# Which rows a partition owns: blocks of 512 consecutive rows against 64 consecutive rows for each partition, in an RMSNorm with SiLU

## The chip, the core and the metric

The kernel runs on one core of one Trainium2 chip. The metric is the device time of one execution in microseconds (us). Smaller is better.

## The reference

The input x has 8 × 1024 rows of 2048 float32 numbers, gamma has 2048, and the output has the shape of x.

```python
rms = np.sqrt(np.mean(x ** 2, axis=-1, keepdims=True) + eps)
out = gamma * x / rms
return (out * (1 / (1 + np.exp(-out)))).astype(np.float32)
```

Each row stands by itself: the mean of its squares gives one factor, the row is multiplied by that factor and by gamma, and SiLU is taken of the product. x and the output have 8192 × 2048 × 4 bytes = 67.1 MB each, and all of it has to be moved once.

## The kernel before

The 8192 rows are cut into nblk = 16 blocks of 512 rows. A block is a tile `xt` of 128 partitions with J = 4 rows on each, that is 8192 float32 numbers or 32 KB for a partition and 4 MB for the tile. Lines 34 to 36 say which rows these are: by the pattern `(b p j) d -> b p (j d)` block b holds rows 512b to 512b + 511, and partition p of it holds rows 512b + 4p to 512b + 4p + 3. So the 4 MB of a block lie in one piece in DRAM, and the 32 KB of partition p + 1 follow those of partition p.

Six tiles exist (BUFS = 6, line 33). Each is loaded, worked on in place and stored from the same place:

- `load(b)`, line 54: one DMA from x to the tile, issued from ScalarE's queue. The first six are issued at the start. Block s of the others is issued inside `squares_scalar(s - 2)`, behind its first Square (line 69), and can start when block s - 6 has been stored, since it takes over that tile.
- `squares_scalar` (line 65) and `squares_vector` (line 73) sum the squares of the four rows, one or two of them on ScalarE and the rest on VectorE.
- `root` (line 82, ScalarE) and `invert` (line 87, VectorE) make the factor of each row.
- `multiply`, line 92: four VectorE instructions multiply a row by its factor and gamma, in place.
- `silu`, line 98: two ScalarE instructions of two rows each, in place; then `store`, line 102, issues one DMA from the tile to the output on SyncE's queue.

The order of the instructions is written out by hand in the loop at line 125; the squares of block b + 1 stand around the product of block b. The last block goes by lines 149 to 156, with four separate SiLU instructions and one store. There is nothing on TensorE but the spreading of gamma over the partitions at the start (line 114). The arithmetic addresses tiles only, never DRAM; the names `xb` and `ob` appear in lines 54 and 102 alone.

Of the kernel before, what the change touches and what calls it, by code (L numbers as in the profile page):

```python
# [1 line left out]

# [4 lines left out]

ACT = mybir.ActivationFunctionType
ALU = mybir.AluOpType


@with_exitstack
def kernel(
    ctx: ExitStack,
    tc: tile.TileContext,
    x: bass.AP,
    gamma: bass.AP,
    eps: bass.AP,
    out: bass.AP,
):  # L20

    nc = tc.nc
    P = nc.NUM_PARTITIONS
    f32 = mybir.dt.float32
    x2 = x.flatten_outer_dims()
    o2 = out.flatten_outer_dims()  # L30
    n, d = x2.shape
    J = 4
    BUFS = 6
    nblk = n // (P * J)
    xb = x2.rearrange("(b p j) d -> b p (j d)", p=P, j=J)
    ob = o2.rearrange("(b p j) d -> b p (j d)", p=P, j=J)

    singles = ctx.enter_context(tc.tile_pool(name="singles", bufs=1))
    pool = ctx.enter_context(tc.tile_pool(name="pool", bufs=BUFS))
    small = ctx.enter_context(tc.tile_pool(name="small", bufs=2))  # L40
    psum = ctx.enter_context(tc.tile_pool(name="psum", bufs=1, space=bass.MemoryType.PSUM))

    Q = 4
    w = d // Q
    g = singles.tile([P, d], f32)
    eps_t = singles.tile([P, 1], f32)
    ones = singles.tile([P, P], f32)
    junk_a = psum.tile([P, d], f32, name="junk_a")
    junk_v = psum.tile([P, d], f32, name="junk_v")
    blocks, sss, rmss, rstds = {}, {}, {}, {}  # L50

    def load(b):
        xt = pool.tile([P, J * d], f32, name="xt")
        nc.scalar.dma_start(out=xt, in_=xb[b])  # L54
        blocks[b] = xt

    def row(b, j):
        return blocks[b][:, j * d:(j + 1) * d]

    def squares_scalar(b, loads=()):  # L60


        sss[b] = small.tile([P, J], f32, name="ss")
        for j in range(share(b)):
            nc.scalar.activation(out=junk_a, in_=row(b, j), func=ACT.Square,  # L65
                                 accum_out=sss[b][:, j:j + 1])
            if j == 0:
                for s in loads:
                    load(s)

    def squares_vector(b):
        for j in range(share(b), J):
            nc.vector.tensor_tensor_reduce(  # L73
                out=junk_v, in0=row(b, j), in1=row(b, j), scale=1.0, scalar=0.0,
                op0=ALU.mult, op1=ALU.add, accum_out=sss[b][:, j:j + 1])

    def share(b):
        return 1 if 4 <= b <= 12 and b % 2 == 0 else 2

    def root(b):  # L80
        rms = small.tile([P, J], f32, name="rms")
        nc.scalar.activation(out=rms, in_=sss.pop(b), func=ACT.Sqrt, scale=1.0 / d, bias=eps_t)  # L82
        rmss[b] = rms

    def invert(b):
        rstd = small.tile([P, J], f32, name="rstd")
        nc.vector.reciprocal(out=rstd, in_=rmss.pop(b))  # L87
        rstds[b] = rstd

    def multiply(b):  # L90
        for j in range(J):
            nc.vector.scalar_tensor_tensor(out=row(b, j), in0=row(b, j), scalar=rstds[b][:, j:j + 1],  # L92
                                           in1=g, op0=ALU.mult, op1=ALU.mult)

    def silu(b):
        for h in range(0, J, 2):
            cols = slice(h * d, (h + 2) * d)
            nc.scalar.activation(out=blocks[b][:, cols], in_=blocks[b][:, cols], func=ACT.Silu)  # L98
        store(b)

    def store(b):
        nc.sync.dma_start(out=ob[b], in_=blocks[b])

    with tc.manual_schedule():

        for b in range(BUFS):
            load(b)
        nc.vector.memset(ones, 1.0)  # L108
        nc.vector.memset(eps_t, float(eps))
        nc.scalar.activation(out=junk_a[:, 0:1], in_=ones[:, 0:1], func=ACT.Square)  # L110
        nc.sync.dma_start(out=g[0:1, :], in_=bass.AP(tensor=gamma.tensor, offset=gamma.offset, ap=[[d, 1], [1, d]]))
        for c in range(Q):
            cols = slice(c * w, (c + 1) * w)
            nc.tensor.matmul(junk_v[:, cols], ones[0:1, :], g[0:1, cols], start=True, stop=True)  # L114
        nc.vector.tensor_copy(out=g, in_=junk_v)  # L115

        last = nblk - 1
        SOON = 3  # L120
        squares_scalar(0)
        squares_vector(0)
        root(0)
        invert(0)
        for b in range(last):
            loads = [b + 3] if BUFS <= b + 3 < nblk else []
            if b < SOON:
                multiply(b)
                squares_scalar(b + 1, loads)
                silu(b)  # L130
                squares_vector(b + 1)
                root(b + 1)
            elif b < last - 1:
                squares_scalar(b + 1, loads)
                squares_vector(b + 1)
                root(b + 1)
                multiply(b)
                silu(b)
            else:
                multiply(b)  # L140
                squares_scalar(b + 1)
                silu(b)
                squares_vector(b + 1)
                root(b + 1)
            if b + 1 < last:
                invert(b + 1)


        for j in range(J):
            if j == J // 2:  # L150
                invert(last)
            nc.vector.tensor_mul(out=row(last, j), in0=row(last, j), in1=g)  # L152
        for j in range(J):
            nc.scalar.activation(out=row(last, j), in_=row(last, j), func=ACT.Silu,  # L154
                                 scale=rstds[last][:, j:j + 1])
        store(last)


# [1 line left out]
_INS = ['x', 'gamma', 'eps']  # L160
_OUTS = [((8, 1024, 2048), 'float32')]

_NUMBERS = {'eps': 9.999999747378752e-06}


# [26 lines left out]
```

## Time and profile before

| | |
|---|---|
| median of 3 runs | 316.96 us (316.75 to 317.02) |
| span of the profiled execution, first to last instruction | 315.0 us |
| median less span: what lies around it | 1.9 us |
| VectorE busy | 235.3 us (75%) |
| ScalarE busy | 213.8 us (68%) |
| DMA packets | 4612, 134.24 MB, mean 426 GB/s |
| loads: issue to landing, median | 38.7 us |
| stores: issue to landing, median | 28.6 us |

The span is cut into 40 slices in the page. In the rows of these slices a digit is the busy share in tenths, and 9 means 90% or more. The row DMA is the mean busy share of the core's 16 DMA engines. DMA queue q10 carries the loads (ScalarE's queue), q1 the stores and gamma (SyncE's queue). A DMA packet is what one DMA engine moves in one go; a block's DMA consists of 128 packets of 32 KB and 16 small ones that signal its end. In the table of windows each row is a stretch of time from the start of the span, with the busy time of each engine in it, the granted TensorE clock, the busy share of the DMA engines and the rate.

### The profile page before, as it was taken

The numbers are of one execution on the slowest core, as the hardware profiler recorded it, in microseconds if no ns is written. First come the engines' busy times: TensorE is split into PE (matmuls) and PEld (weight loads), VectorE is DVE, ScalarE is ACT, GpSimd is POOL, SyncE is SP. The second block draws the span as 40 slices with busy tenths as digits, with TensorE's granted clock in tenths as the row PEclk, the third lists the DMA queues.
The fourth block names the chain that finished last, engine by engine and source line by source line (L and its number), as shares of the span: only waits on it lengthen the run. The fifth ranks groups of instructions, "written<-read, shape, count | busy, mean of one in ns | idle before, by whom it ended". The sixth has DMA issues, their size and how long they took to land.

```text
span 315.0 us, 437 instructions
## 1 busy us (share of the span) xinstructions
PE 7.2 (2%) x8; PEld 2.5 (1%) x8; DVE 235.3 (75%) x157; ACT 213.8 (68%) x136; POOL 0.2 (0%) x4
## 2 busy tenths in 40 slices
PE   6200000000000000000000000000000000000000
PEld 3000000000000000000000000000000000000000
DVE  0679597979995795957959489593996939999600
ACT  1349998972799258782687727877288768779910
POOL 0000000000000000000000000000000000000000
DMA  8999999999999999999999999999999999999996
GB/s 334 399 466 399 399 466 399 466 399 466 399 467 404 459 416 449 420 445 420 445 420 445 420 445 420 445 424 445 420 445 429 437 429 437 429 437 433 433 433 300
DMA packets 4612, 134.24 MB, mean 426 GB/s; under 512 B 513, under 2 KB 513, under 8 KB 513
## 3 DMA queue, kind: packets, MB, share of 16 engines
q10 hardware_dynamic: 2304, 67.11, 49.8%
q1 hardware_dynamic: 2306, 67.12, 49.4%
q14 instruction: 2, 0.02, 0.0%
HBM read 67.12 MB, written 67.11 MB: 426 GB/s over the span
## 4 chain that ended last, share of the span: by engine, by line
DMA 68%; DVE 14%; ACT 11%; issue 2%; ACTq 1%; DVEq 0%
DMA xt<-in_x_dram 68%; DVE xt L92 9%; DVE junk_v L73 5%; ACT xt L98 4%; ACT junk_a L65 3%; ACT xt L154 2%; ACT L82 1%; ACTq L187 1%; ACT L154 0%; ACT L98 0%; ACT rms L82 0%; DVE ss L73 0%; DVE rstd L87 0%; ACTq L54 0%; ACTq L82 0%
## 5 line engine op out<-in xcount | busy, mean ns | idle before, releaser
L92 DVE SCALAR_TENSOR_TENSOR xt<-xt,rstd,g 128x2048 f32<-128x2048 f32 x60 | 137.0, 2345 | 0.1
L98 ACT ACTIVATE xt<-xt 128x4096 f32<-128x4096 f32 x30 | 108.3, 3615 | 27.0 <-DVE xt L92 27.0
L73 DVE CUSTOM_DVE_ANT_0 junk_v<-xt 128x2048 f32<-128x2048 f32 x37 | 85.1, 2299 | 43.0 <-DMA xt<-in_x_dram 42.3
L65 ACT ACTIVATE junk_a<-xt 128x2048 f32<-128x2048 f32 x27 | 50.6, 1876 | 22.8 <-DMA xt<-in_x_dram 22.5
L82 ACT ACT_TABLE_LOAD x15 | 19.2, 1283 | 27.4 <-DVE ss L73 27.3
L98 ACT ACT_TABLE_LOAD x14 | 18.0, 1283 | 0.2
L87 DVE RECIPROCAL rstd<-rms 128x4 f32<-128x4 f32 x16 | 2.7, 171 | 8.4 <-ACT rms L82 8.4
L152 DVE TENSOR_TENSOR xt<-xt,g 128x2048 f32<-128x2048 f32 x4 | 8.9, 2279 | 0.0
L115 DVE COPY g<-junk_v 128x2048 f32<-128x2048 f32 x1 | 2.3, 2292 | 8.6 <-PE junk_v L114 8.6
L82 ACT ACTIVATE rms<-ss,eps_t 128x4 f32<-128x4 f32 x16 | 4.8, 297 | 5.7 <-DVE ss L73 5.5
L154 ACT ACTIVATE xt<-xt,rstd 128x2048 f32<-128x2048 f32 x4 | 7.7, 1990 | 0.0
L114 PE MATMUL junk_v<-g,ones 1*128 1x512 f32 x8 | 7.2, 1073 | 2.4 <-DMA g<-in_gamma_dram 2.4
L73 DVE DVE_READ_ACCUMULATOR2_ANT ss<- 128x1 f32 x37 | 5.2, 140 | 0.0
L65 ACT ACTIVATION_READ_ACCUMULATOR junk_a<-xt 128x1 f32 x27 | 5.0, 186 | 0.0
L110 ACT ACT_TABLE_LOAD x1 | 1.3, 1283 | 3.7 <-issue 3.7
L114 PEld LDWEIGHTS junk_v<-g,ones 1*128 1x128 f32 x8 | 2.5, 326 | 5.5 <-issue 5.5
L154 ACT ACT_TABLE_LOAD x1 | 1.3, 1283 | 0.0
L108 DVE MEMSET ones<- 128x128 f32 x1 | 0.2, 165 | 0.8 <-PEq L173 0.8
L110 ACT ACTIVATE junk_a<-ones 128x1 f32<-128x1 f32 x1 | 0.2, 174 | 0.0
L173 POOL MEMSET const-bfloat16-1.0<- 128x1 bf16 x1 | 0.1, 103 | 0.0
L173 POOL MEMSET const-uint8-127<- 128x1 uint8 x1 | 0.1, 103 | 0.0
L173 POOL MEMSET const-float32-0.0<- 128x1 f32 x1 | 0.1, 99 | 0.2 <-issue 0.2
(2 smaller groups left out, 0.2 us busy)
## 6 DMA issues: line engine op xcount, KB each, us to landing
xt<-in_x_dram ACTq DMA_DIRECT2D x16, 4096.0 KB, 38.7
out_dram<-xt SPq DMA_DIRECT2D x16, 4096.0 KB, 28.6
g<-in_gamma_dram SPq DMA_DIRECT2D x1, 8.0 KB
```

Of the source, the lines that this page charges most:

```text
L65: nc.scalar.activation(out=junk_a, in_=row(b, j), func=ACT.Square, accum_out=sss[b][:, j:j + 1])
L73: nc.vector.tensor_tensor_reduce(out=junk_v, in0=row(b, j), in1=row(b, j), scale=1.0, scalar=0.0, op0=ALU.mult, op1=ALU.add, accum_out=sss ...
L82: nc.scalar.activation(out=rms, in_=sss.pop(b), func=ACT.Sqrt, scale=1.0 / d, bias=eps_t)
L87: nc.vector.reciprocal(out=rstd, in_=rmss.pop(b))
L92: nc.vector.scalar_tensor_tensor(out=row(b, j), in0=row(b, j), scalar=rstds[b][:, j:j + 1], in1=g, op0=ALU.mult, op1=ALU.mult)
L98: nc.scalar.activation(out=blocks[b][:, cols], in_=blocks[b][:, cols], func=ACT.Silu)
L110: nc.scalar.activation(out=junk_a[:, 0:1], in_=ones[:, 0:1], func=ACT.Square)
L114: nc.tensor.matmul(junk_v[:, cols], ones[0:1, :], g[0:1, cols], start=True, stop=True)
L115: nc.vector.tensor_copy(out=g, in_=junk_v)
L152: nc.vector.tensor_mul(out=row(last, j), in0=row(last, j), in1=g)
L154: nc.scalar.activation(out=row(last, j), in_=row(last, j), func=ACT.Silu, scale=rstds[last][:, j:j + 1])
L187: with _tile.TileContext(nc) as tc:
```

## The change

Two lines change. In both patterns the letter p moves to the front, so partition p owns rows 64p to 64p + 63 of x and of the output, and block b takes rows 64p + 4b to 64p + 4b + 3 from it. A block still has 4 rows or 32 KB on each partition, each partition's 32 KB are still one run, and there are still 16 blocks. The runs of neighbouring partitions of one block now lie 64 rows × 8 KB = 512 KB apart; the 32 KB that follow a partition's run belong to the same partition in the next block.

```diff
     J = 4
     BUFS = 6
     nblk = n // (P * J)
-    xb = x2.rearrange("(b p j) d -> b p (j d)", p=P, j=J)
-    ob = o2.rearrange("(b p j) d -> b p (j d)", p=P, j=J)
+    xb = x2.rearrange("(p b j) d -> b p (j d)", p=P, j=J)
+    ob = o2.rearrange("(p b j) d -> b p (j d)", p=P, j=J)
```

## The prediction, made before the changed kernel ran

> **What bounds the kernel now.** I read the 40 slices of the page first.
>
> ```profile
> DVE  0679597979995795957959489593996939999600
> ACT  1349998972799258782687727877288768779910
> ...
> DMA  8999999999999999999999999999999999999996
> ```
>
> VectorE and ScalarE have gaps all through. The DMA engines have none: every slice but the first and the last is full. Then the queues and the bytes:
>
> ```profile
> DMA packets 4612, 134.24 MB, mean 426 GB/s; under 512 B 513, under 2 KB 513, under 8 KB 513
> ## 3 DMA queue, kind: packets, MB, share of 16 engines
> q10 hardware_dynamic: 2304, 67.11, 49.8%
> q1 hardware_dynamic: 2306, 67.12, 49.4%
> ```
>
> The shares of the two queues add up to 99.2% of 16 engines for 315 us. A queue has 16 × 128 = 2048 packets of 32 KB and 16 × 16 = 256 tiny ones. So a load packet takes 0.498 × 16 × 315.0 / 2048 = 1.226 us and a store packet 0.494 × 16 × 315.0 / 2048 = 1.216 us. The trace's packet records, read one by one, say it more sharply: the mean of the loads is 1.2234 us, of the stores 1.2135 us, and more than eight in ten of either kind stand at 1.213 us, which is 32,768 B / 1.2135 us = 27.0 GB/s for one engine and 432 GB/s for 16. At nearly every moment from 2 to 313 us, 15 or 16 packets are in the air.
>
> Third, the windows, to see where this rate isn't reached, and the work that lies beside it:
>
> ```profile
> core 0: us, PE busy (x) PEld busy (x) DVE busy (x) ACT busy (x) POOL busy (x), PEclk, DMA share, GB/s
> 2.00:12.00 10.00, 7.16 (x8) 2.49 (x8) 2.29 (x1) 1.46 (x2) 0.00 (x0) 1.00 0.91 387
> 12.00:32.00 20.00, 0.00 (x0) 0.00 (x0) 17.02 (x12) 14.76 (x13) 0.00 (x0) 1.00 1.03 444
> 32.00:44.00 12.00, 0.00 (x0) 0.00 (x0) 8.71 (x7) 11.91 (x9) 0.00 (x0) 1.00 0.97 396
> 100.00:140.00 40.00, 0.00 (x0) 0.00 (x0) 29.95 (x20) 26.88 (x17) 0.00 (x0) 1.00 1.00 434
> 220.00:260.00 40.00, 0.00 (x0) 0.00 (x0) 30.23 (x21) 26.48 (x17) 0.00 (x0) 1.00 1.00 433
> ```
>
> Loads alone (12:32) and loads mixed with stores (100:140) both run at about 435 GB/s. (A packet counts where it is recorded, so a short window can be off by some per cent either way.) Two stretches are slow. By the packet records, 16 packets of the first block, one for each engine, take 1.25 to 2.25 us, which lifts the block's mean to 1.299 us. Where the first store joins the loads, at 36 to 38 us, 21 load packets take 1.28 to 1.89 us, and block 3, loaded then, has a mean of 1.293 us. The stores that join there stand at 1.213 us.
>
> The chain of waits is the last view; this is the middle of it:
>
> ```profile
> 66.81 37.73 DMA xt<-in_x_dram
> 104.56 38.95 DMA xt<-in_x_dram
> 143.54 38.66 DMA xt<-in_x_dram
> 182.23 38.68 DMA xt<-in_x_dram
> ```
>
> A load lands 38.7 us after its issue. A block's load and a block's store take 2 × 8 × 1.2135 = 19.4 us of an engine, so a load has about a block's load and store queued ahead of it. The compute engines wait for data, and the queues are never dry.
>
> **The sum before.** An engine moves 128 load packets and 128 store packets. First packet at 1.75 us; 128 × (1.2234 + 1.2135) = 311.9 us; from the last packet's end at 313.70 to the end of the span at 315.03, 1.3 us. Together 1.75 + 311.9 + 1.3 = 315.0, the span of this execution. The median of the runs, 316.96, lies 1.93 above the span, and I carry those 1.93 along.
>
> **The change part by part.** Instructions, semaphores, tiles, order and issues: nothing is added, removed or moved. A load is issued in 0.33 us and a store in 0.33 us by the trace, 16 of each, and stays so. The runs are 32 KB before and after; that the trace shows 2048 packets of 32 KB to a queue, although a block of before is one piece of 4 MB, says that the packets are already cut by partition. So I count the same 4096 data packets, at no cost.
>
> What changes is the DRAM address of each packet, thus perhaps its duration. The compute beside it covers any lengthening: in 40 us, 2.07 blocks, VectorE is busy 29.95 us, so it needs 14.5 us of a block's 19.4 and longer packets only give it more rest. Nor does a later landing start a new wait: loads are issued two blocks ahead and the queue they stand in would be the bound still. If packets became *shorter*, VectorE would be next, at 14.5 us a block, a quarter away. So the whole price is 128 × (lengthening of a load + lengthening of a store).
>
> No row of before shows runs 512 KB apart, so this price is bounded from both sides.
> - Below: a packet at 1.2135 us is the fastest any block had. If every load came to it, the gain would be 128 × (1.2234 − 1.2135) = 1.3 us. That needs the cold start and the joining of the stores to go away, which no address explains; a gain much under that is not excluded.
> - No price: in the steady state 16 engines, loads from x and stores to the output beside each other, stand at 1.213 us without scatter. The runs that they hold at one time are already whole multiples of 32 KB apart.
> - Above: the slowest block of loads in the trace, 1.299 us. All loads at that: 128 × (1.299 − 1.2234) = 9.7 us. Stores as well: 128 × (1.299 − 1.2135) = 10.9 us more, 20.6 us together.
>
> For stores I take no lengthening: those that met slowed loads at 36 to 38 us stayed at 1.213. For loads I take the middle of 1.2234 and 1.299, 1.261 us. The steady state isn't a near row, since there the runs of a block are neighbours in DRAM, and the slow blocks aren't, since in them one packet or two out of eight is long and the others are as always. That is 128 × 0.0378 = 4.8 us, and 316.96 + 4.8 = **321.8 us**.
>
> A rule speaks against this change. The Trainium skill, "DMA: Bandwidth & Descriptors", in "Latency and other measured facts", reports copies of tiles of 128 partitions whose rows lie a large power of two apart: 207 GB/s per direction at 512 KiB, 164 at 2 MiB, 103 at 4 MiB, and 214 when the pitch is padded by 4 KiB. It calls its explanation, that streams in step fall on the same channels of the memory, an inference. By its ratio of 214 to 207 the time would be an estimated 316.96 × 1.034 = 327.7 us; by the steady rows above it would not move. No row of this trace shows the pitch, so no run here shows it yet.
>
> **The rivals.**
>
> *Loads and stores both lengthen.* The new addresses are the same for both directions. For it: nothing in the change favours loads. Against it: the stores of before kept their time where loads lost theirs. From 326.6 (all loads at 1.299) to 337.6 us (stores too), more if packets get longer than the slowest block of before; the mark is a store mean above 1.23 us.
>
> *Nothing moves (not slower).* The bound is the DMA engine's own 27.0 GB/s, and the memory behind it delivers in any order of addresses without holding an engine up. For it: the exact 1.213 us of nearly all packets, in loads alone and in loads with stores, means that the engines and not the memory set the pace, so there is room before the memory counts. It decides as long as the mean packet lengthens by under 0.63 / 256 = 2.5 ns. Then 317.0 us.
>
> *A little faster.* The joining of the stores at 36 us and the cold start lose 1.3 us together. If the new addresses remove them, 315.7 us. Against it: both are bound to a moment, not to an address, and half of it must go before it can be told.
>
> *The change doesn't do what it says*, in that packets are cut otherwise than by partition: it would show in another packet count. I give it no chance of its own.
>
> **How the numbers follow.** The lean to a loss comes from the rows: nearly all packets stand at their floor, so new addresses can lengthen them and hardly shorten them; the trace has packets up to 1 us over it, and a mean of 2.5 ns over it would be told already. About 0.2% (0.63 us) is what a measurement of this kernel can tell from no change. Loads lengthen, 317.6 to 326.6 us: 0.53. Both lengthen, above 326.6: 0.18. Nothing moves: 0.22. Faster: 0.07. So slower 0.71, same 0.22, faster 0.07. The range starts at 316.3, the lower edge of no change, and ends at 332.1, the middle of the second case: left out are the 0.07 of faster and somewhat over half of 0.18, about 0.18 in all. The forecast case's own range is 317.6 to 326.6.
>
> **What would show it.** The page after should have 4612 packets, 134.24 MB, and DMA slices of 9 throughout. If I am right, q10's share of the engines rises above q1's: 1.261 against 1.2135, or about 50.4% to 48.5% of a span near 320; the windows from 100 to 260 us fall from 434 to some 425 GB/s; VectorE's and ScalarE's busy times stay at 235 and 214 us. If the windows stay at 434, nothing moved. If q1's share rises as well, both lengthen. Slices of the DMA row below 9 in the middle would say that the queues ran dry, which none of my cases has. A rate above 434 would make the whole reading wrong, for the engine's pace then was no floor.

## The result: 1.1% slower, and the profile after

The changed kernel takes 320.32 us (median of 4 runs, 319.68 to 321.78) against 316.99 us for the kernel before beside it: a ratio of 1.0112, 95% interval 1.0097 to 1.0128. The profiled execution took 320.55 us with a span of 318.8 us, 3.7 us more than the span before.

The page of the changed kernel, in the rows that were read of the kernel before (40 slices, bytes, queues):

```profile
DVE  0579597979796595956969479594895939999600
ACT  1249998971797358782587827867278768679920
...
DMA  8999999999999999999999999999999999999995
...
DMA packets 4612, 134.24 MB, mean 421 GB/s; under 512 B 513, under 2 KB 513, under 8 KB 513
## 3 DMA queue, kind: packets, MB, share of 16 engines
q10 hardware_dynamic: 2304, 67.11, 49.7%
q1 hardware_dynamic: 2306, 67.12, 48.8%
```

The packets and bytes are the same to the last one, and the DMA engines are as full as before. The two shares hardly moved, but they are shares of a longer span: a load packet is now 0.497 × 16 × 318.8 / 2048 = 1.238 us, a store packet 0.488 × 16 × 318.8 / 2048 = 1.215 us. The packet records (here and below those of one execution of each kernel) say 1.2377 and 1.2139 us, against 1.2234 and 1.2135 before. So loads got longer and stores hardly.

The windows of the changed kernel (stretch, its length, busy time of PE, PEld, DVE, ACT and POOL, granted clock, DMA share, GB/s):

```profile
40.00:80.00 40.00, 0.00 (x0) 0.00 (x0) 36.42 (x25) 28.75 (x20) 0.00 (x0) 1.00 1.00 426
80.00:120.00 40.00, 0.00 (x0) 0.00 (x0) 32.07 (x22) 27.72 (x17) 0.00 (x0) 1.00 1.00 431
120.00:160.00 40.00, 0.00 (x0) 0.00 (x0) 30.82 (x22) 26.96 (x17) 0.00 (x0) 1.00 1.01 432
160.00:200.00 40.00, 0.00 (x0) 0.00 (x0) 30.97 (x21) 27.11 (x17) 0.00 (x0) 1.00 1.00 431
200.00:240.00 40.00, 0.00 (x0) 0.00 (x0) 30.64 (x21) 26.19 (x17) 0.00 (x0) 1.00 1.00 432
240.00:280.00 40.00, 0.00 (x0) 0.00 (x0) 30.49 (x22) 30.71 (x19) 0.00 (x0) 1.00 1.00 433
295.00:305.00 10.00, 0.00 (x0) 0.00 (x0) 5.10 (x4) 9.46 (x7) 0.00 (x0) 1.00 0.94 406
```

Two of the same windows of the kernel before:

```profile
40.00:80.00 40.00, 0.00 (x0) 0.00 (x0) 36.42 (x26) 28.34 (x20) 0.00 (x0) 1.00 1.00 433
295.00:305.00 10.00, 0.00 (x0) 0.00 (x0) 1.28 (x1) 5.68 (x4) 0.00 (x0) 1.00 1.02 442
```

The loss isn't spread evenly. From 40 to 80 us the rate is 426 GB/s, and by 240 it is back at 433; the kernel before had 432 or 433 in every one of these windows from 40 to 280 us. The packet records give the same by load blocks. The table below has the mean length of a load packet of each block in ns; the excess is what the 2048 load packets take over 1.213 us each, the length of nearly all packets, divided by 16 engines.

| | block 0 | 1 and 2 | 3 | 4 | 5 | 6 to 10 | 11 to 15 | excess |
|---|---|---|---|---|---|---|---|---|
| before | 1299 | 1213 | 1293 | 1213 | 1213 | 1213 | 1213 | 1.33 us |
| after | 1307 | 1213 | 1346 | 1271 | 1235 | 1219 to 1234 | 1216 to 1224 | 3.16 us |

Blocks 1 and 2 are loaded while no store is under way, and are untouched. The loss begins in block 3, where the first store joins, and fades. Block 3 is long before as well, and in the kernel with 256 KB below, which loses no time, it has 1351 ns; what sets the changed kernel apart is the blocks from 4 on, which hold 1.34 of the 1.83 us that the excess grew by.

One thing more stands in the records. The excess rose by 1.83 us an engine, the span by 3.7. A DMA is done when the last of the engines is, and the engines no longer end together. (The records don't name the engine; a packet is put to the engine whose packet ended just before it.) Before, their last packets end from 312.95 to 313.70 us, 313.23 on the mean; after, from 315.12 to 317.57, 315.72 on the mean. The mean end moved by 2.5 us (most of it the 1.83 of excess, and pauses of 0.2 to 0.9 us on half of the engines), the last end by 3.87. The window from 295 to 305 us, with a DMA share of 0.94, has a part of the pauses in it: six engines that were ahead had emptied their queues when the last store was issued, at 304.5 us, two more did before its first packets started at 305.4. That issue itself is late because the last load landed at 282.8 us instead of 279.0; the 21.7 us of work between that landing and the issue are the same in both. The slowest engine had packets queued all the time.

### The profile page after: what moved, and what is told of

Its sections match the earlier page's. It is cut to its first block, busy times and chain, and to the rows that moved or that the text cites. A ratio compares the mean times of both kernels' runs of the same rounds, so it can differ in the third digit from the quotient of the medians.

```text
span 318.8 us, 437 instructions
## 1 busy us (share of the span) xinstructions
PE 7.2 (2%) x8; PEld 2.5 (1%) x8; DVE 235.3 (74%) x157; ACT 213.7 (67%) x136; POOL 0.2 (0%) x4
## 2 busy tenths in 40 slices
DMA packets 4612, 134.24 MB, mean 421 GB/s; under 512 B 513, under 2 KB 513, under 8 KB 513
## 4 chain that ended last, share of the span: by engine, by line
DMA 68%; DVE 14%; ACT 11%; issue 2%; ACTq 1%; DVEq 0%
DMA xt<-in_x_dram 68%; DVE xt L92 9%; DVE junk_v L73 5%; ACT xt L98 4%; ACT junk_a L65 3%; ACT xt L154 2%; ACT L82 1%; ACTq L187 1%; ACT L154 0%; ACT L98 0%; ACT rms L82 0%; DVE ss L73 0%; DVE rstd L87 0%; ACTq L54 0%; ACTq L82 0%
```

## The experiments

Three theories went in. A: runs of one block at a distance of 512 KB hold each other up, in either direction. B: it takes loads and stores that meet at the same places, so both patterns. C: any jump of an engine's addresses between packets costs. In the results "late excess" is the excess of load packets from 45 us on, after the first store has joined: 0.00 us an engine before, 1.34 after. Each ratio is to the kernel before, run beside it (medians 316.91 to 317.00 us); the changed kernel itself was not run again beside these.

**One direction alone: load_far.**

```diff
-    ob = o2.rearrange("(p b j) d -> b p (j d)", p=P, j=J)
+    ob = o2.rearrange("(b p j) d -> b p (j d)", p=P, j=J)
```

> Loads go by the new pattern, stores by the old one; each row is computed as before but written to another place of the output, so the rows come out in another order. Theory A (the pitch of 512 KB: runs of one block at such a distance hold each other up, in either direction, and the loads show it): the load packets lengthen by about half of what they do with both changed (block 3 about 1.32 us, blocks 4 to 8 about 1.22 to 1.24) and the time is about 318.6 us. Theory B (it is loads and stores that meet at the same places, which takes both patterns): load packets as before from block 4 on (1.213 us), 317.0 us. Theory C (what costs is that a load engine jumps 512 KB between packets): all of the loss, 320.3 us.

Measured: 318.72 us, ratio 1.0056 (1.0044 to 1.0068). The share of its load queue, and a span of 316.6 us, give 0.498 × 16 × 316.6 / 2048 = 1.232 us for a load packet; by the records 1.2309, and 1.2135 for stores. Its queues:

```profile
q10 hardware_dynamic: 2304, 67.11, 49.8%
q1 hardware_dynamic: 2306, 67.12, 49.1%
```

**The other alone: store_far.**

```diff
-    xb = x2.rearrange("(p b j) d -> b p (j d)", p=P, j=J)
+    xb = x2.rearrange("(b p j) d -> b p (j d)", p=P, j=J)
```

> Stores go by the new pattern, loads by the old one; the rows come out in another order. Theory A: about half of the loss, 318.6 us, shown by load packets of blocks 3 to 8, since loads wait and stores do not. Theory B: 317.0 us. Theory C: loads as before, 317.0 us, store packets at 1.2135 us.

Measured: 318.19 us, ratio 1.0035 (1.0021 to 1.0049), with one of its six runs, 317.12 us, as fast as the kernel before. Its queues:

```profile
q10 hardware_dynamic: 2304, 67.11, 49.7%
q1 hardware_dynamic: 2306, 67.12, 49.2%
```

Load packets take 1.2260 us by the records, stores 1.2135. The mean alone doesn't tell, since the kernel with 256 KB below has 1.2261 us and loses nothing. But 12 load packets after 45 us take 1.23 to 1.64 us, where the kernel before has none, although only the stores' addresses changed. So load packets carry the loss whichever direction is spread.

By time, theory A was close (318.6 expected twice) and B and C fall. By the packets A missed and B has a part: the late excess is 0.19 us with loads spread and 0.13 with stores spread, far less than half of 1.34, and blocks 4 to 8 of load_far have means of 1.214 to 1.220 us where A had 1.22 to 1.24. So most of the late lengthening takes both. (Not all: in load_far 22 packets of blocks 1 and 2, loaded before any store, take 1.23 to 1.32 us.) The times still rise by 1.7 and 1.2 us. With loads spread, the engines end 1.1 us later than before on the mean; 0.95 us of that is excess, 0.56 of it in block 3, and the slowest engine ends 1.1 us behind the mean, at 315.40 us. With stores spread, the rise is the work of single engines: the engines end at 313.52 us on the mean, 0.3 us later than before; but one of them, with four long load packets of 1.48 to 1.64 us between 155 and 275 us, ends at 315.15 us, and the span follows it.

**Another distance: pitch256 and pitch480.** In the first, two groups of 4096 rows, so that runs lie 256 KB apart:

```diff
-    xb = x2.rearrange("(p b j) d -> b p (j d)", p=P, j=J)
-    ob = o2.rearrange("(p b j) d -> b p (j d)", p=P, j=J)
+    C = 2
+    xb = x2.rearrange("(c p b j) d -> c b p (j d)", c=C, p=P, j=J)
+    xb = [xb[c, b] for c in range(C) for b in range(nblk // C)]
+    ob = o2.rearrange("(c p b j) d -> c b p (j d)", c=C, p=P, j=J)
+    ob = [ob[c, b] for c in range(C) for b in range(nblk // C)]
```

> Both patterns with two groups of 4096 rows, in each of which a partition owns 32 consecutive rows: runs of a block are 256 KB apart instead of 512 KB, all else as in the changed kernel. Theories A and B (distance in powers of two decides): a smaller loss, between 317.0 and 319 us, load mean between 1.2234 and 1.2377. Theory C (any jump costs): 320.3 us as at 512 KB.

In the second, 60 rows a partition, 480 KB:

```diff
-    xb = x2.rearrange("(p b j) d -> b p (j d)", p=P, j=J)
+    R = (nblk - 1) * P * J
+    xb = x2[0:R, :].rearrange("(p b j) d -> b p (j d)", p=P, j=J)
+    xb = [xb[b] for b in range(nblk - 1)] + [x2[R:n, :].rearrange("(p j) d -> p (j d)", p=P, j=J)]
...
```

> Both patterns with 60 consecutive rows a partition for the first 15 blocks (runs of a block 480 KB apart, not a power of two), and the last block in one piece. Theories A and B: the loss is gone, 317.0 us, load packets of blocks 4 to 14 at 1.213 us. Theory C: 320 us, load packets long as at 512 KB.

Measured: 317.03 us at 256 KB (ratio 1.0004, 0.9995 to 1.0013) and 316.91 us at 480 KB (0.9997, 0.9988 to 1.0005). No load packet after 45 us is longer than 1.23 us in either; after the change there are 98. From the page of the 480 KB kernel, bytes and queues:

```profile
DMA packets 4612, 134.24 MB, mean 426 GB/s; under 512 B 513, under 2 KB 513, under 8 KB 513
## 3 DMA queue, kind: packets, MB, share of 16 engines
q10 hardware_dynamic: 2304, 67.11, 49.8%
q1 hardware_dynamic: 2306, 67.12, 49.4%
```

These are the lines of the kernel before, digit for digit. The runs of a block lie 480 KB apart here and nothing is lost, so C is out, and so is a large distance by itself: 480 KB costs nothing, 512 KB does. That 512 KB costs because it is a power of two isn't shown, since 256 KB is one as well and is free. This is the clearest pair of the study. Neither is faster than the kernel before, whose engines already run packet on packet.

**Out of step: stagger.**

```diff
+    late = singles.tile([P, 1792], f32)
     with tc.manual_schedule():
+        for start, count in ((0, 8), (8, 8), (32, 4), (36, 4), (64, 2)):
+            nc.sync.dma_start(out=late[start:start + count, :], in_=x2[start:start + count, 0:1792])
```

> The changed kernel with five small DMAs ahead of everything on SyncE's queue (7 KB rows of x to a tile that nothing reads; 8, 8, 4, 4 and 2 partitions). They should keep 8 of the 16 DMA engines busy for 0, 4 for about 0.5, 2 for about 1.0 and 2 for about 1.3 us longer than the others, so that the engines don't walk their runs in step. Theory A in its form with step (engines in step collide, and each collision sets them apart, which is why the loss of the changed kernel fades from 1.06 us in load block 3 to 0.02 in block 15): the load excess from 45 us on, 1.34 us an engine in the changed kernel, falls to under 0.7; the time still carries up to 1.3 us of the added DMAs, so 318.5 to 320 us. If step doesn't matter (the fading has another cause): excess from 45 us on stays at 1.2 to 1.5, time 320.5 to 322 us.

Measured: 321.76 us, ratio 1.0166 (1.0143 to 1.0190); the runs lie between 321.2 and 323.7 us, and the profiled one is one of the two longest, 323.50 us. The engines were apart: they finish load block 2 over 2.4 us, against 0.9 in the changed kernel. The late excess is 1.45 us, not under 0.7, and 0.58 us of excess on stores came with it; the engines end from 314.65 to 320.43 us. The form of theory A in which engines in step collide, and a collision sets them apart, is not borne out. It doesn't fade here either: load block 12 still has a mean of 1.246 us. Why the loss of the changed kernel fades stays open.

**Larger distances: halves512, halves1m, quarters2m, and a control, halvesnear.** To get more than 512 KB, a block was cut into two or four DMAs of 64 or 32 partitions:

```diff
-    xb = x2.rearrange("(p b j) d -> b p (j d)", p=P, j=J)
+    H = 2
+    xb = x2.rearrange("(q h b j) d -> b h q (j d)", h=H, q=P // H, j=J)
...
-        nc.scalar.dma_start(out=xt, in_=xb[b])
+        for h in range(H):
+            nc.scalar.dma_start(out=xt[h * (P // H):(h + 1) * (P // H), :], in_=xb[b, h])
```

with `(h q b j)` for halves512, `(b h q j)` for halvesnear and H = 4 for quarters2m, and the stores likewise.

> Control for the next: every load and store is issued as two DMAs of 64 partitions each (2 MB), with the rows of the changed kernel, so runs of one DMA lie 512 KB apart. If the cut in two costs nothing, theory A gives 320.3 us as in the changed kernel, give or take 1 us since engines now take other partitions.

> Two DMAs of 64 partitions as in the control, but partition q of the first half and partition q of the second own neighbouring 64-row pieces, so runs of one DMA lie 1 MB apart. Theory A: a larger loss than at 512 KB, since 256 KB gave none and 512 KB gave 3.3 us: 323 to 335 us, load packets longer through all blocks. If the 512 KB loss were the whole effect of leaving the old order: the same as the control.

> Four DMAs of 32 partitions each, partition owners dealt out so that runs of one DMA lie 2 MB apart. Theory A: a larger loss again, 330 to 410 us. By the Trainium skill (DMA: Bandwidth & Descriptors, Latency and other measured facts), 164 GB/s per direction at 2 MiB against 214 would be an estimated 413 us. If the loss doesn't grow with the distance: 320 to 321 us.

> Control for the kernels cut into DMAs of 64 and 32 partitions: the rows of the kernel before, each load and store issued as two DMAs of 64 partitions, so runs of one DMA lie 32 KB apart. If the cut itself made 450 us of them (two engines then share what one had on the side of the tile: load packets of 2.5 us alone): 440 to 455 us here too. If the distance made it: about 317 us.

Measured: 450.36 us at 512 KB (440.22 to 482.48), 444.97 at 1 MB (439.43 to 451.06), 466.52 at 2 MB (462.06 to 483.12), and 451.08 us (447.82 to 454.91) in the control with runs 32 KB apart. So the cut makes the 450 us and not the distance; the control answers it, and these kernels say nothing on whether a larger distance costs more in whole DMAs. (The cut in four has no control of its own.) The windows of halvesnear, loads alone:

```profile
12.00:32.00 20.00, 0.00 (x0) 0.00 (x0) 4.89 (x5) 0.00 (x0) 0.00 (x0) 1.00 1.01 208
32.00:44.00 12.00, 0.00 (x0) 0.00 (x0) 0.00 (x0) 0.00 (x0) 0.00 (x0) 1.00 1.02 213
```

The engines are full and move half as much: a load packet of 32 KB takes 2.53 us there instead of 1.213.

**The transfers by themselves: copy_near, copy_far, copy_far16.** All the arithmetic on x is left out of both kernels; copy_far16 has J = 2 and BUFS = 12:

```diff
-        last = nblk - 1
...
-        store(last)
+        for b in range(nblk):
+            store(b)
+            if b + BUFS < nblk:
+                load(b + BUFS)
```

> The kernel before without its arithmetic: each block is stored as it was loaded, so the output is x itself. The same 4096 packets of 32 KB. Stores join at about 13 us. The DMA engines stay the bound: 316 to 317.5 us, load packets from block 2 on at 1.213 us.

> The changed kernel without its arithmetic (output is x). If the loss is the memory's and the engines' own (theory A): 1 to 6 us above copy_near, with long load packets and stores at 1.2135. If it takes the compute's timing of stores (rival D: the moments at which stores are issued, late and singly, make the collisions): within 0.7 us of copy_near. The Trainium skill's 207 against 214 GB/s per direction (DMA: Bandwidth & Descriptors, Latency and other measured facts) would make copy_near's time 3.4% longer, an estimated 327 us.

> As copy_far, with runs of 16 KB (two rows) instead of 32 KB, 32 blocks of 2 MB and 12 tiles; the distance stays 512 KB. If each start of a run can collide: about twice the loss of copy_far. If the loss goes by bytes: the same as copy_far, give or take 1 us.

Measured: 317.06 us (ratio 1.0004, 0.9995 to 1.0012), 319.75 us (1.0124, 1.0079 to 1.0169; two of its six runs at 323.6) and 318.85 us (1.0061, 1.0048 to 1.0074). Copying alone takes what the whole kernel takes, so the arithmetic was hidden in full, and the loss is there without it: copy_far has a late excess of 0.82 us and copy_near none. It doesn't need the kernel's timing of the stores (rival D). One window of copy_near, then the same of copy_far (its lowest of the four from 20 to 180 us):

```profile
100.00:140.00 40.00, 0.00 (x0) 0.00 (x0) 0.00 (x0) 0.00 (x0) 0.00 (x0) 1.00 1.00 433
100.00:140.00 40.00, 0.00 (x0) 0.00 (x0) 0.00 (x0) 0.00 (x0) 0.00 (x0) 1.00 1.00 427
```

The third was expected wrongly. With runs of 16 KB no load packet is held up once the stores have joined. Its slices and queues:

```profile
GB/s 309 362 431 433 431 433 431 431 433 431 431 431 431 433 431 431 431 431 435 433 431 431 431 431 431 431 431 431 431 431 433 431 433 433 431 433 431 433 431 331
...
q10 hardware_dynamic: 4608, 67.11, 50.0%
q1 hardware_dynamic: 4610, 67.12, 49.5%
```

The rate is flat from the third slice on, and every load block but the first two has a mean of 0.611 us in the records (the cold start lengthens the first, the joining of the stores the second, as in copy_near). What it loses against copy_near is every packet's share: 512 × 0.611 = 312.8 us for an engine against 256 × 1.2135 = 310.7, 2.2 us, where 1.8 were measured. That this is the packets' size is inferred from its evenness; no run has 16 KB runs side by side. The distance of 512 KB alone, then, isn't the cause of long packets either; with runs of 16 KB none after the second block takes over 0.62 us.

## Why the prediction was right, and where it was off

**The bound held.** The queues stayed full up to the pauses from 294 us on, the packets stayed 4612, VectorE and ScalarE kept 235.3 and 213.7 us, and no new wait decided. The copies confirm it from outside: 317.06 us without any arithmetic. That loads lengthen and stores don't, taken from the joining of the first store, was right too, and store_far shows it most plainly, where only stores moved and only loads got longer. It isn't so in every kernel: in stagger the stores had 0.58 us of excess.

**The size was right partly by luck, by two errors that cancel in part.** The term 128 × 0.0378 = 4.8 us took the middle between no lengthening and the slowest block of before. The load packets went from 1.2234 to 1.2377 us, not 1.261: 128 × 0.0143 = 1.83 us. By the sum as it was made, this would have given 318.8 us. The other half of the measured 3.3 us comes from a term that the sum lacked: it worked with mean packets, but the end is that of the slowest engine. The spread of the ends grew from 0.75 to 2.45 us, and the last end lies 1.85 us behind the mean end instead of 0.47. In the kernel before that term was small, since all engines ran alike, and the sum hid it: 1.75 + 311.9 = 313.7 us fell on the last end although it was made of means, while the mean end was 313.23. The term grew when packets lengthened unevenly over the engines.

**The row for the price.** I held neither the steady state nor the slow blocks of before to be near the new layout, and took the middle. The steady state was the nearer: blocks 5 to 15 lie at 1216 to 1235 ns, against 1213 before. The loss is at its highest where the first store joins (block 3: 1293 before, 1346 after, beyond the 1299 that I had as the slowest), and the windows fell to 426 only at the start and 431 to 433 later, where I had named 425 throughout.

**The rivals.** "Both lengthen" fell, with the stores at 1.2139 us. "Nothing moves" fell in the changed kernel, but it is what the times show at 256 and 480 KB. "A little faster" fell: neither the cold start nor the join went away.

**The rule of the Trainium skill** ("DMA: Bandwidth & Descriptors", "Latency and other measured facts"). It had the right sign. A remedy that it names is a pitch padded by a few KiB; pitch480, 32 KB short of 512 KB, lost nothing at 316.91 us, and no run here tried so small a padding. Its size was not met. 207 against 214 GB/s would have been an estimated 327.7 us; the runs show 320.32 for the kernel, 319.75 for the copy, and 318.85 for the copy with 16 KiB runs, the size that the page's figure is for, where no load packet is held up after the second block. The page's copies run between HBM tensors, and it doesn't say whether they pass through a tile as those here do. Whether it is the memory that holds the packets up, and which part of it, the runs don't show.

**What stays open.** What sets 512 KB apart from 256 and 480 KB, why it takes 32 KB runs as well, why the loss fades in the kernel, and what a whole DMA with runs more than 512 KB apart would cost.

## What to carry to other kernels

Where the DMA engines are full packet on packet, look at the mean length of the load packets and at the spread of the engines' last ends: the mean tells what a packet costs, and the slowest engine sets the time. A layout that gives each partition a long piece of DRAM was free at 256 and 480 KB and cost 1.1% at 512 KB, so try it with another distance before giving it up. Compare the transfers alone, without arithmetic, first: two copy kernels showed the loss at once.

## What the runs showed of the hardware that I had not expected

- The direction that is spread isn't the one that gets longer: with only stores at 512 KB, 12 load packets after 45 us took 1.23 to 1.64 us, where there were none before, and stores stayed at 1.2135.
- A block moved as two DMAs of 64 partitions instead of one of 128 went at 199 to 213 GB/s instead of about 435 when loads ran alone, in all three layouts in DRAM that were tried, and the kernel took 451 us instead of 317 with the layout of before.
- A packet of 16 KB takes 0.611 us, 0.7% more for a byte than one of 32 KB at 1.2135, and held its time at a distance of 512 KB where the larger did not. It was run at that distance alone.
